# Where the hidden tiles' transposing transfers and joining copies stand in a streamed FFN, and where the rotation table lives

## The chip, the cores and the metric

One core of a Trainium2 chip runs the whole block as one program. The metric is the device time of one execution, in microseconds. Before the change it is 2484.98 us, the median of three runs between 2484.42 and 2486.36.

## The reference

One transformer layer over 256 rows of width 2048, everything in float32:

```python
h = layer_norm(ALPHA * h + 0.5 * swiglu_ffn(h, ffn1_w_in[l], ffn1_w_out[l]), ...)
mix = hybrid_mixer(h, w_in[l], gate_bias[l], rel_bias[l], ..., cos, sin)
h = layer_norm(ALPHA * h + mix, ...)
xa = memory_cross_attention(h, mem, ...)
h = layer_norm(ALPHA * h + xa, ...)
h = layer_norm(ALPHA * h + 0.5 * swiglu_ffn(h, ffn2_w_in[l], ffn2_w_out[l]), ...)
...
def swiglu_ffn(x, w_in, w_out):
    g, u = jnp.split(x @ w_in, 2, axis=-1)
    return (jax.nn.silu(g) * u) @ w_out
```

The hidden width is 5504, 43 blocks of 128. The mixer holds a chunked attention and a latent attention whose queries and key are turned by a rotation table (`cos`, `sin`).

## The kernel before

**Streaming the weights.** All weights come from HBM once. SyncE (SP) loads tiles `raw` of 128 x 2048 float32, 1 MB each, into three buffers (line 185). Each matmul operand is a pair: ScalarE (ACT) rounds the tile into `hi`, in two instructions of 1024 columns (line 248, in `halves`), VectorE (DVE) subtracts to get the rest, `lo` (line 251), and TensorE (PE) multiplies hi by hi, hi by lo and lo by hi, summing in PSUM. A tile `raw` is free for the next load when VectorE's subtraction has read it.

**An in-group of the FFN.** `ffn` (from line 534) goes over the hidden width in groups of four blocks of 128 columns; `F_SPLIT` makes two halves of 24 and 19 blocks, so six groups and then five, the last of which is 384 columns wide rather than 512. A group makes gate and up for 256 rows in `pair_group`, in eight steps numbered 0 to 7, each with a weight tile of its own. Steps 0, 1, 3, 5 and 7 are plain: 24 matmuls of `mm_pair` (line 295). Steps 2, 4 and 6 are *sums steps* (`mm_sums`, line 349): 21 matmuls over sums of weights (made by VectorE, lines 233 and 235, in a block called `H` and rounded into a block called `X`) into four PSUM banks of their own. After step 6 `shared` (lines 651 to 656) empties these banks: two copies of ScalarE, then two adds, a subtraction and another add or subtraction of VectorE; the next group's plain banks and sums banks trade places with them, so the next group's step 0 writes into the banks that `shared` has emptied.

**The hidden tile's way.** At the group's end `product` (in `hidden`) adds the sums results to the plain banks, takes SiLU and multiplies; the product is 256 x 512. It has to become a matmul operand, so it must be transposed. Per 128 rows (`tt` = 0, 1): ScalarE copies the float32 words apart into upper and lower 16-bit halves (line 709), a transposing transfer turns them (line 711, a DMA that ScalarE issues into its own queue, q10), and later `turn` joins the halves again (the *join*, line 716, on ScalarE) and splits the result into hi and lo of a block `H` (lines 240 and 241). After the six, and after the five groups, the out phase multiplies these H blocks with `w_out`.

**The order of the work.** The program is a list of items. `weave` puts side items between the main items of a group: `turn` of the group before stands ahead of main item 3 of the next group (or of the out phase, after a half's last group). Counted in main items, `shared` is one of them, so item 3 is step 3. `run` goes through the list and issues loads, roundings and subtractions of weights ahead of their use; a priority then places instructions within each engine's order, which is fixed when the program is built:

```python
self.weave(main, {3: [turn]} if turn else {}, prio=0)     # an in-group
...
side = {3: [turn]}                                        # an out phase
```

**The rest.** The first group of the first FFN takes the input from other loads; `load_rest` (line 515) then loads `h`, `vecs` and the rotation table `rope` (128 x 512 float32, 256 KB) on SP's queue at the third group. `rope` stays in a constant tile to the end and is read in two places of the mixer: `kpe` (lines 948, 949) and `rope_q` (line 1048). Work tiles `w2` of 128 x 512 words have five buffers; the product, its halves and the four results of `shared` are such tiles.

Of the kernel before, what the change touches and what calls it, by code (L numbers as in the profile page):

```python
# [94 lines left out]
class Kernel:  # L95
# [32 lines left out]
    def w2(self, shape=(P, 512), dt=F32):  # L128
        return self.work.tile(list(shape), dt, tag="w2", bufs=5, name=self.name("w2"))

# [41 lines left out]
    def run(self):  # L172
# [44 lines left out]

        done = 0
        for fn, ws, held, prio in self.items:
            need = done + len(ws)  # L220
            while nxt < len(queue) and ahead(need, held):
                live += slots(queue[nxt])
                ready.append(load(nxt))
                nxt += 1
            got = [ready.pop(0) for _ in ws]
            live -= sum(slots(queue[done + i]) for i in range(len(ws)))
            done = need
            with self.prio(prio):
                fn(*got)
# [13 lines left out]
    def halves(self, src, hi, lo):  # L243

        n = src.shape[1]
        for c in range(0, n, 1024):
            d = min(c + 1024, n)
            self.nc.scalar.copy(hi[:, c:d], src[:, c:d])  # L248

        with self.tc.issue_after(self.chain.ins) if self.chain is not None else nullcontext():  # L250
            self.nc.vector.tensor_tensor(lo[:, :n], src, hi[:, :n].bitcast(F32), ALU.subtract)  # L251
        return hi, lo
# [194 lines left out]
    def setup(self):  # L447
        nc, t = self.nc, self.t
        self.ones = self.w1((P, P))
        nc.vector.memset(self.ones, 1.0)  # L450
        nc.scalar.activation(self.sm("first", 1, bufs=1), self.ones[:, 0:1], AF.Silu)
        self.vecs = self.const.tile([P, N_VEC], F32, name="vecs")
        self.rope = self.const.tile([P, 2, S], F32, name="rope")
        self.ident = self.const.tile([P, P], F32, name="ident")
        make_identity(nc, self.ident)
        self.mask = self.const.tile([P, 3 * P], F32, name="mask")
        nc.gpsimd.memset(self.mask, 0.0)
        self.mask_out(self.mask)
        self.krope = self.const.tile([P, 2, S], F32, name="krope")
        nc.gpsimd.memset(self.krope, 0.0)  # L460
        self.h = [self.res.tile([P, D], F32, tag=f"h{i}", name=f"h{i}") for i in range(2)]
# [53 lines left out]
    def load_rest(self):  # L515
        nc, t = self.nc, self.t
        with self.tc.issue_after(self.last_load.ins):
            for tt in range(2):
                nc.sync.dma_start(self.h[tt], t["x"][tt])
            nc.sync.dma_start(self.vecs, t["vecs"])  # L520
            nc.sync.dma_start(self.rope, t["rope"])

# [8 lines left out]
    def ffn(self, tag, xT, st, first=None, steps=None, late=None, before=None, tags=None):  # L531
# [6 lines left out]
        for half, nf in enumerate(F_SPLIT):  # L538
# [3 lines left out]
            for g in range(-(-nf // 4)):  # L542
# [9 lines left out]
                else:  # L552
                    src = t[tag + "_w_in"][j] if n == 4 else t[tag + "_w_in_r"][0]
                    main = self.collect(self.pair_group, bank, src, n * P, KT, xT, SUMS_IN, fx, ps, qs, None, SUM_HOME + ("H5",))
                self.weave(main, {3: [turn]} if turn else {}, prio=0)
                for c, (home, _) in homes.items():
# [24 lines left out]

            side = {3: [turn]}
            for c, (home, k) in homes.items():
                if home == "X0":
                    side[4 + 2 * k] = [form(c)]
            if not end:
# [101 lines left out]
    def hidden(self, ps, j, g, n, hid, qs):  # L688
# [4 lines left out]
        def words(v):  # L693
            return v.bitcast(U16)

        def product():
            for tt in range(2):
# [7 lines left out]
                else:  # L705
# [4 lines left out]
                               words(s[tt]).rearrange("p (c k) -> p k c", k=2))  # L710
                nc.scalar.dma_start_transpose(words(s[tt]).rearrange("p (b q) -> p b q", q=P), words(u[tt]))

        def turn():
            hid.blocks += self.act([f"H{g}"]).blocks
            for tt in range(2):
                nc.scalar.copy(words(u[tt]).rearrange("p (c k) -> p k c", k=2),
                               words(s[tt]).rearrange("p (k c) -> p k c", k=2))
                hi, lo = (hid.blk(a, 4 * g, n)[:, :, tt * P:(tt + 1) * P] for a in (0, 1))
                self.split(u[tt].rearrange("p (i q) -> p i q", i=n), hi, lo)
        return product, turn  # L720

# [103 lines left out]
    def mixer(self, xT, st, steps):  # L825
# [109 lines left out]
        def kpe(w):  # L935
            both = w[0].rearrange("p (k m) -> p k m", k=KT)
            with self.prio(SOON):
                nc.scalar.copy(both[:, :, 64:], w[1].rearrange("p (k m) -> p k m", k=KT)[:, :, 64:].bitcast(F32))
            ps = self.at_tile()
            for kt in range(KT):  # L940
# [6 lines left out]
            swap(c, a, nc.gpsimd)  # L947
            nc.vector.tensor_tensor(a, a, self.rope[:, 0, :], ALU.mult)
            nc.vector.tensor_tensor(c, c, self.rope[:, 1, :], ALU.mult)
            for j in range(2):  # L950
# [80 lines left out]

        rope_items = []
        for g in range(2):
            def fn(w, g=g):
                if g == 0:
                    self.rt = self.block("T0")
                for j in range(4):
                    ps = self.mm_tile()
# [3 lines left out]
            def rope_q(g=g):  # L1042
# [4 lines left out]
                for v, k in ((r, 0), (sw, 1)):  # L1047
                    nc.vector.tensor_tensor(v, v, self.rope[:, k:k + 1, :].to_broadcast([P, 4, S]), ALU.mult)
                nc.vector.tensor_tensor(r, r, sw, ALU.add)
# [476 lines left out]
```

## Time and profile before

| what | value |
|---|---|
| median of three runs | 2484.98 us |
| the profiled execution | 2484.44 us |
| its span in the trace | 2482.6 us |
| mean granted clock of TensorE | 0.996 |
| busy time of TensorE | 2450.8 us, 99% of the span |
| busy time of VectorE | 2096.0 us, 84% |
| busy time of ScalarE | 1449.5 us, 58% |
| busy time of GpSimd (POOL) | 36.0 us, 1% |
| moved by the DMA engines | 501.42 MB, 202 GB/s |

The span runs from the first instruction to the last; the execution's own time is 1.84 us longer. Busy time counts instructions that compute; issuing a DMA and waiting do not count. An engine name with a q (ACTq, SPq) is the sequencer of that engine, where it issues DMAs. In lists of waits, an arrow with a name after idle time says what ended it. The granted clock is the share of its full rate at which TensorE was let run in a stretch of time.

### The profile page before, as it was taken

Reading aid. Unit: us, or ns where it says so; the run is one execution under the profiler, and the core shown is the slowest. Engines: PE = TensorE matmul, PEld = TensorE weight load, DVE = VectorE, ACT = ScalarE, POOL = GpSimd, SP = SyncE. Lnnn points to the kernel's source line nnn. Section 1 sums busy time; section 2 is a strip of 40 time slices with the busy share of each in tenths; the row PEclk is TensorE's granted clock in tenths of the full one; section 3 lists DMA queues with packets and bytes.
Section 4 is the critical chain, followed back from the end, with each engine's and each line's share of the span. In section 5 each row is a group of like instructions: output and inputs, shape, how many; then the busy total and the mean of one; then the engine's idle time right before and its main releaser. Section 6 shows DMA issues by size and latency. Waiting matters only on the chain.

```text
span 2482.6 us, 30056 instructions
## 1 busy us (share of the span) xinstructions
PE 2450.8 (99%) x11603; PEld 2052.7 (83%) x11603; DVE 2096.0 (84%) x2392; ACT 1449.5 (58%) x1932; POOL 36.0 (1%) x78
## 2 busy tenths in 40 slices
PE   9999999999999999999999999999999999999998
PEld 7788888888888888888888888898888888888976
DVE  8899989998878897788788798558878999889986
ACT  6667655766555556556455565545566665566652
POOL 0000000000000001000000000000000000000000
PEclk9999999999999999999999999999999999999999
DMA  7767556667645666554466557544556765666764
GB/s 265 222 220 207 197 203 228 209 202 194 230 177 203 212 212 210 183 165 152 163 232 223 187 174 250 187 161 152 196 195 204 229 216 208 220 202 211 243 191 142
DMA packets 118528, 501.42 MB, mean 202 GB/s; under 512 B 53904, under 2 KB 54672, under 8 KB 63216
## 3 DMA queue, kind: packets, MB, share of 16 engines
q1 hardware_dynamic: 67632, 468.94, 55.2%
q10 hardware_dynamic: 46304, 12.46, 3.1%
q0 software_dynamic: 4448, 18.09, 2.2%
q8 instruction: 91, 1.49, 0.2%
q14 instruction: 53, 0.43, 0.0%
HBM read 484.77 MB, written 2.10 MB: 196 GB/s over the span
## 4 chain that ended last, share of the span: by engine, by line
PE 91%; DVE 3%; DMA 3%; ACT 2%; issue 1%; ACTq 0%; DVEq 0%
PE mm L295 23%; PE at L295 23%; PE mm L349 10%; PE at L349 10%; PE mm L261 9%; PE mm L282 7%; PE mm L263 4%; DMA w<-w 2%; PE at L976 1%; PE at L282 1%; DVE lo L251 1%; ACT hi L248 1%; DVE X L251 1%; PE at L815 0%; PE at L1017 0%
## 5 line engine op out<-in xcount | busy, mean ns | idle before, releaser
L248 ACT CAST hi<-raw 128x1024 fp32r<-128x1024 f32 (+1 forms) x852 | 803.9, 984 | 529.8 <-PE at L295 175.5
L251 DVE TENSOR_TENSOR lo<-raw,hi 128x2048 fp32r<-128x2048 f32 (+1 forms) x427 | 905.5, 2122 | 197.4 <-ACT hi L248 194.7
L295 PE MATMUL mm<-hi,T 128*128 128x512 f32 (+1 forms) x1232 | 286.3, 383 | 0.0
L295 PEld LDWEIGHTS mm<-hi,T 128*128 128x128 f32 x1232 | 229.1, 188 | 43.3 <-DVE w L656 0.4
L295 PE MATMUL at<-hi,T 128*128 128x512 f32 x1072 | 255.8, 389 | 1.1 <-ACT hi L248 1.1
L248 ACT CAST X<-H 128x1024 fp32r<-128x1024 f32 (+1 forms) x166 | 170.2, 1034 | 139.4 <-DVE H L233 86.9
L295 PEld LDWEIGHTS at<-hi,T 128*128 128x128 f32 x1072 | 201.0, 188 | 43.8 <-ACT hi L248 2.0
L251 DVE TENSOR_TENSOR X<-H,X 128x2048 fp32r<-128x2048 f32 (+1 forms) x83 | 186.9, 2252 | 56.9 <-ACT X L248 56.0
L295 PE MATMUL at<-hi,H 128*128 128x512 f32 x592 | 144.5, 396 | 9.0 <-ACT hi L248 7.5
L295 PE MATMUL mm<-lo,T 128*128 128x512 f32 (+1 forms) x616 | 147.8, 382 | 0.0
L295 PEld LDWEIGHTS at<-hi,H 128*128 128x128 f32 x592 | 113.1, 192 | 34.4 <-ACT hi L248 8.4
L295 PE MATMUL at<-lo,T 128*128 128x512 f32 x536 | 133.0, 389 | 1.4 <-DVE lo L251 1.4
L295 PEld LDWEIGHTS mm<-lo,T 128*128 128x128 f32 x616 | 114.6, 188 | 20.9
L261 PE MATMUL mm<-T,hi 128*128 128x512 f32 x512 | 123.7, 393 | 0.0
L295 PEld LDWEIGHTS at<-lo,T 128*128 128x128 f32 x536 | 100.5, 188 | 22.6 <-DVE lo L251 1.8
L235 DVE TENSOR_TENSOR H<-H,raw 128x512 f32<-128x512 f32 (+1 forms) x166 | 112.5, 678 | 1.9
L261 PEld LDWEIGHTS mm<-T,hi 128*128 128x128 f32 x512 | 93.8, 188 | 19.1 <-issue 0.7
L295 PE MATMUL mm<-hi,H 128*128 128x512 f32 x448 | 108.0, 391 | 0.0
L233 DVE TENSOR_TENSOR H<-raw 128x1024 f32<-128x1024 f32 (+1 forms) x83 | 99.6, 1200 | 6.4 <-DMA raw<-ffn_w_in 5.4
L295 PEld LDWEIGHTS mm<-hi,H 128*128 128x128 f32 x448 | 83.6, 188 | 17.2 <-DVE w L270 0.2
L349 PE MATMUL mm<-X,X 128*128 128x512 f32 x348 | 92.4, 391 | 0.4 <-DVE X L251 0.4
L349 PE MATMUL at<-X,X 128*128 128x512 f32 (+1 forms) x315 | 82.0, 387 | 2.8 <-DVE X L251 2.8
(330 smaller groups left out, 4048.0 us busy)
## 6 DMA issues: line engine op xcount, KB each, us to landing
raw<-ffn_w_in SPq DMA_DIRECT2D x150, 1024.0 KB, 4.9
raw<-ffn_w_out SPq DMA_DIRECT2D x66, 1024.0 KB, 4.8
raw<-w_gate SPq DMA_DIRECT2D x32, 1024.0 KB, 4.8
raw<-ffn_w_out_r SPq DMA_DIRECT2D x16, 1024.0 KB, 4.9
raw<-w_qk SPq DMA_DIRECT2D x16, 1024.0 KB, 4.8
raw<-w_o_b SPq DMA_DIRECT2D x16, 1024.0 KB, 4.8
raw<-w_out SPq DMA_DIRECT2D x16, 1024.0 KB, 4.9
raw<-w_xk SPq DMA_DIRECT2D x16, 1024.0 KB, 4.9
```

The lines of the kernel that those rows point to most:

```text
L233: self.nc.vector.tensor_tensor(two[0], two[1], raw[:, :m].unsqueeze(1).to_broadcast([P, 2, m]), ALU.add)
L235: self.nc.vector.tensor_tensor(t[:, a * m:a * m + m], t[:, b * m:b * m + m], raw[:, a * m:a * m + m], ALU.add)
L248: self.nc.scalar.copy(hi[:, c:d], src[:, c:d])
L251: self.nc.vector.tensor_tensor(lo[:, :n], src, hi[:, :n].bitcast(F32), ALU.subtract)
L261: self.nc.tensor.matmul(ps, hi[j], x.both(kt), start=(j == 0), stop=False)
L263: self.last_mm = self.nc.tensor.matmul(ps[:, :S], lo[j], x.at(0, kt), start=False, stop=(j == n - 1))
L282: self.last_mm = self.nc.tensor.matmul(ps, x.at(xi, kt)[:, tt * P:(tt + 1) * P], w[wi][:, j * 512 + c:j * 512 + c + m], start=(start and j ...
L295: self.last_mm = self.nc.tensor.matmul(ps[tt, g][:, :n], x.at(xi, kt)[:, tt * P:(tt + 1) * P], w[wi][:, c:c + n], start=first and j + wi + ...
L349: self.last_mm = self.nc.tensor.matmul(bank[:, :m], a[xi], v[wi][:, c * m:(c + 1) * m], start=own and first and wi + xi == 0, stop=own and ...
L976: nc.tensor.matmul(ps[:, c0:c0 + nk], q[:, tt * P:(tt + 1) * P], k[:, :nk], start=(j == 0), stop=(j == len(parts) - 1))
```

## The change

It has three parts.

1. **The transposing transfers** leave `product` for an item of their own, `send`, that stands ahead of main item 2 of the next group, and SP issues them (line 719 of the new kernel) into the queue of the weight loads (q1), not ScalarE into q10.
2. **`turn`** moves from ahead of main item 3 to ahead of main item 6, which is step 6. Each of its joins (now line 725) is also ordered behind the last rounding of the weight that the next main item uses, `next_hi`; where that item is step 6, this is the seventh weight of the group, and the last rounding is that of its sums (into a block `X`). In the out phases `send` and `turn` take the same places 2 and 6 among other main items.
3. **The rotation table** loses its constant tile and its load in `load_rest`. `rotation()` takes a `w2` tile and has GpSimd load the 256 KB into it, once in `kpe` and once for each of the two rotation items of the queries. `w2` gets a sixth buffer.

Other line numbers rise by two to five: the rounding is line 250, its subtraction 253, the split into H 242 and 243, the plain matmuls 297, the sums matmuls 351, `shared` 656 to 661, the copy apart 714.

```diff
-        return self.work.tile(list(shape), dt, tag="w2", bufs=5, name=self.name("w2"))
+        return self.work.tile(list(shape), dt, tag="w2", bufs=6, name=self.name("w2"))
...
-        done = 0
+        done, highs = 0, []
         for fn, ws, held, prio in self.items:
             need = done + len(ws)
             while nxt < len(queue) and ahead(need, held):
                 live += slots(queue[nxt])
                 ready.append(load(nxt))
+                highs.append(self.last_hi)
                 nxt += 1
             got = [ready.pop(0) for _ in ws]
             live -= sum(slots(queue[done + i]) for i in range(len(ws)))
             done = need
+            self.next_hi = highs[min(done, nxt - 1)] if highs else None
...
-            self.nc.scalar.copy(hi[:, c:d], src[:, c:d])
+            self.last_hi = self.nc.scalar.copy(hi[:, c:d], src[:, c:d])
...
-            nc.sync.dma_start(self.rope, t["rope"])
+
+    def rotation(self):
+        r = self.w2((P, 2, S))
+        self.nc.gpsimd.dma_start(r, self.t["rope"])
+        return r
...
-                self.weave(main, {3: [turn]} if turn else {}, prio=0)
+                self.weave(main, turn or {}, prio=0)
...
-            side = {3: [turn]}
+            side = dict(turn)
             for c, (home, k) in homes.items():
                 if home == "X0":
-                    side[4 + 2 * k] = [form(c)]
+                    side[4 + 2 * k] = side.get(4 + 2 * k, []) + [form(c)]
...
-                nc.scalar.dma_start_transpose(words(s[tt]).rearrange("p (b q) -> p b q", q=P), words(u[tt]))
+
+        def send():
+            for tt in range(2):
+                nc.sync.dma_start_transpose(words(s[tt]).rearrange("p (b q) -> p b q", q=P), words(u[tt]))
 
         def turn():
             hid.blocks += self.act([f"H{g}"]).blocks
             for tt in range(2):
-                nc.scalar.copy(words(u[tt]).rearrange("p (c k) -> p k c", k=2),
-                               words(s[tt]).rearrange("p (k c) -> p k c", k=2))
+                with self.tc.issue_after(self.next_hi.ins):
+                    nc.scalar.copy(words(u[tt]).rearrange("p (c k) -> p k c", k=2),
+                                   words(s[tt]).rearrange("p (k c) -> p k c", k=2))
                 hi, lo = (hid.blk(a, 4 * g, n)[:, :, tt * P:(tt + 1) * P] for a in (0, 1))
                 self.split(u[tt].rearrange("p (i q) -> p i q", i=n), hi, lo)
-        return product, turn
+        return product, {2: [send], 6: [turn]}
```

In `kpe` and `rope_q` the reads of `self.rope` become reads of the tile that `rotation()` returned, called at the start of `kpe`'s work and of each query projection item.

The built programs show what stands where on each engine (line, operation, output<-input, tile shape of a partition count and a count of elements; `x2` is two such rows in a row). **First place**: ScalarE between the second group's product and the third group's weights. `hi_844`, `hi_880`, `hi_916` of before (`hi_840`, `hi_876`, `hi_914` now) are the roundings of the third group's weights of steps 2, 3 and 4, `w_108` to `w_111` hold the second group's product and its halves, `H_138` is its H block, and `X_123` takes the rounded weight sums. Before:

```order
L709 COPY w_108_753<-w_109_754 128x1024
L709 COPY w_110_755<-w_111_756 128x1024
L711 DMA_TRANSPOSE w_109_754<-w_108_753 128x8x128
L711 DMA_TRANSPOSE w_111_756<-w_110_755 128x8x128
L248 CAST hi_844<-raw_794 128x1024
L248 CAST hi_844<-raw_794 128x512
L248 CAST X_123_849<-H_116_796 128x1024 x2
L716 COPY w_108_753<-w_109_754 128x2x512
L248 CAST hi_880<-raw_878 128x1024 x2
L240 CAST H_138_926<-w_108_753 128x4x128
L716 COPY w_110_755<-w_111_756 128x2x512
L248 CAST hi_916<-raw_885 128x1024
```

and now:

```order
L250 CAST hi_840<-raw_793 128x1024
L714 COPY w_108_752<-w_109_753 128x1024
L250 CAST hi_840<-raw_793 128x512
L714 COPY w_110_754<-w_111_755 128x1024
L250 CAST X_123_845<-H_116_795 128x1024
L250 CAST hi_876<-raw_874 128x1024 x2
L250 CAST X_123_845<-H_116_795 128x1024
L250 CAST hi_914<-raw_881 128x1024
L250 CAST hi_914<-raw_881 128x512
```

The two issues and the two joins with their first split have left this place; the copies apart stand among roundings. SP at the same place, from the load of `raw_794` (now `raw_793`) on; before:

```order
L185 DMA raw_794<-ffn_w_in 128x2048
L519 DMA h_102<-x 128x2048
L519 DMA h_103<-x 128x2048
L520 DMA vecs<-vecs 128x136
L521 DMA rope<-rope 128x512
L185 DMA raw_878<-ffn_w_in 128x2048
L185 DMA raw_885<-ffn_w_in 128x2048
L185 DMA raw_957<-ffn_w_in 128x2048
```

and now:

```order
L185 DMA raw_793<-ffn_w_in 128x2048
L520 DMA h_101<-x 128x2048
L520 DMA h_102<-x 128x2048
L521 DMA vecs<-vecs 128x136
L185 DMA raw_874<-ffn_w_in 128x2048
L185 DMA raw_881<-ffn_w_in 128x2048
L719 DMA_TRANSPOSE w_109_753<-w_108_752 128x8x128
L719 DMA_TRANSPOSE w_111_755<-w_110_754 128x8x128
L185 DMA raw_948<-ffn_w_in 128x2048
```

The table's load is gone and the two transposing transfers stand between the loads of two weights. **Second place** on ScalarE and VectorE, **the third piece shown**: the end of step 6 in the fifth group, where `shared` (copies of `w_251` and `w_252`) now meets the joins of the group before (`w_203` to `w_206`, into `H_247`). `X_243` (now `X_242`) are the rounded sums of step 6, `hi_1652` (now `hi_1643`) is the rounding of step 7's weight, `hi_1680` (now `hi_1678`) and `hi_1721` (now `hi_1719`) are those of steps 0 and 1 of the next group. ScalarE before:

```order
L248 CAST X_243_1621<-H_240_1591 128x1024
L248 CAST hi_1652<-raw_1650 128x1024
L248 CAST X_243_1621<-H_240_1591 128x1024
L248 CAST hi_1652<-raw_1650 128x1024
L248 CAST hi_1680<-raw_1678 128x1024
L651 COPY w_251_1685<-at_1516 128x512
L248 CAST hi_1680<-raw_1678 128x1024
L652 COPY w_252_1686<-at_1517 128x512
L248 CAST hi_1721<-raw_1719 128x1024 x2
```

and now:

```order
L250 CAST X_242_1612<-H_239_1582 128x1024
L250 CAST hi_1643<-raw_1641 128x1024
L725 COPY w_203_1371<-w_204_1372 128x2x512
L656 COPY w_251_1683<-at_1514 128x512
L242 CAST H_247_1648<-w_203_1371 128x4x128
L725 COPY w_205_1373<-w_206_1374 128x2x512
L250 CAST hi_1678<-raw_1676 128x1024
L657 COPY w_252_1684<-at_1515 128x512
L242 CAST H_247_1648<-w_205_1373 128x4x128
L250 CAST hi_1678<-raw_1676 128x1024
L250 CAST hi_1719<-raw_1717 128x1024 x2
```

Two joins and two roundings into H are new beside the two copies, and one half of `hi_1678` comes later than the half of `hi_1680` did. VectorE now, behind the subtraction of step 7's weight:

```order
L253 TENSOR_TENSOR lo_1644<-raw_1641,hi_1643 128x2048
L243 TENSOR_TENSOR H_247_1648<-w_203_1371,H_247_1648 128x4x128
L658 TENSOR_TENSOR w_253_1685<-w_251_1683,at_1516 128x512
L659 TENSOR_TENSOR w_252_1684<-w_252_1684,w_253_1685 128x512
L243 TENSOR_TENSOR H_247_1648<-w_205_1373,H_247_1648 128x4x128
L660 TENSOR_TENSOR w_253_1685<-w_253_1685,at_1517 128x512
L661 TENSOR_TENSOR w_254_1686<-w_252_1684,at_1517 128x512
L253 TENSOR_TENSOR lo_1679<-raw_1676,hi_1678 128x2048
```

The two splits into H (line 243) are new here and stand ahead of the first add and between the second and the third of the four instructions that empty the banks. The joins stand at such a place in 18 of the 22 groups; the other four are in the out phases, where the blocks of a half's last group are joined.

More of the change, by code (lines that the diff above doesn't have):

```diff
@@ L452, in setup @@
         self.vecs = self.const.tile([P, N_VEC], F32, name="vecs")
-        self.rope = self.const.tile([P, 2, S], F32, name="rope")
         self.ident = self.const.tile([P, P], F32, name="ident")
@@ L938, in kpe @@
                 nc.scalar.copy(both[:, :, 64:], w[1].rearrange("p (k m) -> p k m", k=KT)[:, :, 64:].bitcast(F32))
+            rope = self.rotation()
             ps = self.at_tile()
@@ L947, in kpe @@
             swap(c, a, nc.gpsimd)
-            nc.vector.tensor_tensor(a, a, self.rope[:, 0, :], ALU.mult)
-            nc.vector.tensor_tensor(c, c, self.rope[:, 1, :], ALU.mult)
+            nc.vector.tensor_tensor(a, a, rope[:, 0, :], ALU.mult)
+            nc.vector.tensor_tensor(c, c, rope[:, 1, :], ALU.mult)
             for j in range(2):
@@ L1029, in a_out @@
             self.add(fn)
-        rope_items = []
+        rope_items, rot = [], {}
         for g in range(2):
@@ L1036, in fn @@
                     self.rt = self.block("T0")
+                rot[g] = self.rotation()
                 for j in range(4):
@@ L1047, in rope_q @@
                 for v, k in ((r, 0), (sw, 1)):
-                    nc.vector.tensor_tensor(v, v, self.rope[:, k:k + 1, :].to_broadcast([P, 4, S]), ALU.mult)
+                    nc.vector.tensor_tensor(v, v, rot[g][:, k:k + 1, :].to_broadcast([P, 4, S]), ALU.mult)
                 nc.vector.tensor_tensor(r, r, sw, ALU.add)
```

## The prediction

> **What bounds the kernel now.** I read the page first, then the waits of TensorE, then the lines that send and use the moved transfers, then the timeline around them. The page comes first: busy time, share of the span, instruction count, and below it the shares of the chain that ended last.
>
> ```profile
> span 2482.6 us, 30056 instructions
> PE 2450.8 (99%) x11603; PEld 2052.7 (83%) x11603; DVE 2096.0 (84%) x2392; ACT 1449.5 (58%) x1932; POOL 36.0 (1%) x78
> PE 91%; DVE 3%; DMA 3%; ACT 2%; issue 1%; ACTq 0%; DVEq 0%
> ```
>
> TensorE is the bound: it is idle for 2482.6 - 2450.8 = 31.8 us only. An edit on ScalarE or on a queue can therefore win only what lies in these idle places, and in matmuls that ran slowly behind them. The change touches one line with a wait of its own, the transposing transfers (line 711), which the joining copies (line 716) wait for:
>
> ```profile
> L711 ACTq DMA_TRANSPOSE w<-w x44: 1227/1249/2820, 56.1 to 2371.7; - x44
>   ACT w L716: 26.9, 9
> DMA to landing us min/median/max: 3.0/4.4/16.6
> ```
>
> Issuing one holds ScalarE for about 1.25 us, it lands after 3.0 to 16.6 us, and ScalarE stands 26.9 us before joins. Does TensorE pay for that? The timeline (start, duration, engine, line; in brackets the idle time before it and who ended it) shows three places where it does, and two plain pieces to compare with:
>
> ```profile
> 109.13 3.79 PE L295 MATMUL mm<-hi,T 128*128 128x512 f32 x16
> 115.11 1.33 ACT L716 COPY w<-w 128x1024 uint16<-128x1024 uint16 x1 [6.58 <-DMA w<-w]
> 117.92 0.73 PE L349 MATMUL mm<-hi,T 128*128 128x512 f32 x2 [3.18 <-ACT hi L248]
> 125.96 3.80 PE L295 MATMUL mm<-hi,T 128*128 128x512 f32 x16
> ...
> 216.64 0.62 PE L349 MATMUL mm<-hi,T 128*128 128x512 f32 x2
> 221.40 3.79 PE L295 MATMUL mm<-hi,T 128*128 128x512 f32 x16
> ...
> 613.81 1.04 ACT L716 COPY w<-w 128x768 uint16<-128x768 uint16 x1 [7.13 <-DMA w<-w]
> 616.63 5.54 PE L295 MATMUL at<-hi,H 128*128 128x512 f32 x16 [4.18 <-ACT hi L248]
> 2388.43 5.51 PE L295 MATMUL at<-hi,H 128*128 128x512 f32 x16 [3.35 <-ACT hi L248]
> ```
>
> ScalarE waits 6.58 and 7.13 us for a transpose, the rounding (line 248) of the next weight is queued behind that join, and TensorE waits for this rounding. Sixteen matmuls then take 5.54 and 5.51 us where 3.79 is usual, and the sums step from 117.92 lasts until 125.96, 8.04 us, where the one from 216.64 lasts 4.76. The windows of these stretches (columns: length, busy time and count of each engine, granted clock, DMA share, GB/s) say why:
>
> ```profile
> 118.70:122.10 3.40, 3.40 (x9) 2.58 (x8) 3.36 (x5) 2.19 (x3) 0.00 (x0) 0.50 0.05 19
> 126.00:130.00 4.00, 4.00 (x19) 3.33 (x18) 4.00 (x4) 1.22 (x2) 0.00 (x0) 1.00 0.49 147
> 617.10:620.40 3.30, 3.30 (x10) 2.52 (x9) 3.15 (x4) 2.84 (x4) 0.00 (x0) 0.50 0.00 0
> 2388.60:2392.00 3.40, 3.40 (x9) 2.63 (x10) 3.25 (x4) 3.14 (x4) 0.00 (x0) 0.50 0.00 0
> ```
>
> After each of the three waits the granted clock is 0.50 for some 3.4 us and 1.00 afterwards, so each wait is paid about one and a half times.
>
> **Part 1, the three stalls.** Wait plus lengthening: 3.18 + (8.04 - 4.76) = 6.46 us; 4.18 + (5.54 - 3.79) = 5.93; 3.35 + (5.51 - 3.79) = 5.07. Together 17.46 us. In the new order no rounding is queued behind a join that still waits: the transposes go out behind the third step and the join stands behind the seventh weight's rounding, over four steps later. A plain step is 226.84 - 221.40 = 5.44 us (row below), so some 20 us lie between, more than the longest landing of 16.6. I book the whole 17.46.
>
> By the Trainium skill (TensorE: Matmul & The Clock Gate, HAM oscillation) idle gaps have to exceed about 3.4 us before the clock is halved. The trace differs: 3.18 and 3.35 us were enough. By the rule only the wait of 4.18 would have been charged the slow clock, and some 5 us of the sum would be of another origin and might stay.
>
> **Part 2, why the transposes were late, and whether SP's queue carries them.** Median landing of a weight load, the three loads issued from 98.9 to 110.4 us, the two queues, and what SP's queue waits for:
>
> ```profile
> raw<-ffn_w_in SPq DMA_DIRECT2D x150, 1024.0 KB, 4.9
> DMA to landing us min/median/max: 9.5/12.6/16.2
> q1 hardware_dynamic: 67632, 468.94, 55.2%
> q10 hardware_dynamic: 46304, 12.46, 3.1%
> SPq L185 <- DVE lo L251: 1503.8, 294, 15.3
> ```
>
> Beside the slow transposes the weight loads, usually 4.9 us, took 9.5 to 16.2: both wait on each other. The transposes of q10 are 46304 small packets (12.46 MB) that share the 16 DMA engines with q1. In one queue I take them to run one behind the other: 3.0 us each, the shortest landing. SP has room for the issues: it waits 1503.8 us in all for VectorE to free a raw tile. What stands behind them is the next weight load: at worst it is late by two issues (2.5 us) and two transposes (6.0 us). Below nothing too: a load no longer slowed from 4.9 to 16.2 gains up to 11.3 us. I take zero, nearest to the row of 4.9, since a load is late only after the joins have left ScalarE's way. The tightest place is the short last group (384 wide), where SP comes to the transposes before they are ready:
>
> ```profile
> L185 SPq DMA_DIRECT2D raw<-ffn_w_out x1: 328/328/328, 596.1 to 596.1; - x1
> 596.98 1.56 ACT L709 COPY w<-w 128x768 uint16<-128x768 uint16 x2
> ```
>
> That load must now follow copies that end at 598.54 and two issues, so it goes out near 600.5 and lands by 605.4 to 611.4 (0 or 6.0 us of transposes ahead of it). Its matmuls are those that would start at 616.63 - 4.18 = 612.45; rounding takes 2 us, so the stall is 0 to 1 us. I take 0.
>
> The Trainium skill (DMA: Bandwidth & Descriptors, Issuing engines are not separate DMA queues) speaks against a gain here: the issuing engine saves sequencer time only, and all transfers interleave on the same DMA engines. Its section on queues, rings and completion order says that a DMA engine takes turns between queues packet by packet but consumes one ring in order, which fits the rows above; by the first sentence alone the late loads would stay, which is the first rival.
>
> **Part 3, ScalarE without the issues.** 44 issues of 1.25 us leave ScalarE, 55 us, but it is 58% busy; only the first group shows TensorE behind them:
>
> ```profile
> 59.36 1.06 ACT L248 CAST X<-H 128x1024 fp32r<-128x1024 f32 x1 [2.33 <-issue]
> 61.41 1.20 PE L295 MATMUL at<-hi,T 128*128 128x512 f32 x4 [0.91 <-ACT hi L248]
> 67.49 0.72 PE L295 MATMUL at<-lo,T 128*128 128x512 f32 x2 [1.38 <-DVE lo L251]
> ```
>
> The 2.33 us go. Of the 0.91 + 1.38 = 2.29 us between 0 and 2.29 return, since VectorE's chain follows; I take 1.5.
>
> **Part 4, the joins in their new place.** They now meet the four copies and adds that empty the shared banks (lines 651 to 656 of before) between step 7's rounding and the next group's first step, in 18 of 22 groups. Rows of such a place, and the durations of a join copy and of the rounding into H:
>
> ```profile
> 217.69 2.00 ACT L248 CAST hi<-raw 128x1024 fp32r<-128x1024 f32 x2
> 219.59 0.58 ACT L651 COPY w<-at 128x512 f32<-128x512 f32 x1
> 220.03 2.28 DVE L251 TENSOR_TENSOR lo<-raw,hi 128x2048 fp32r<-128x2048 f32 x1
> 222.23 0.68 DVE L653 TENSOR_TENSOR w<-w,at 128x512 f32<-128x512 f32 x1
> 226.84 3.79 PE L295 MATMUL at<-hi,T 128*128 128x512 f32 x16
> ...
> L716 ACT COPY w<-w x44: 1043/1358/1373, 63.2 to 2385.6; 128x1024 uint16<-128x1024 uint16 x40, 128x768 uint16<-128x768 uint16 x4
> L240 ACT CAST H<-w x72: 401/612/634, 65.6 to 2386.9; 128x512 fp32r<-128x512 f32 x44, 128x256 fp32r<-128x256 f32 x24, 128x384 fp32r<-128x384 f32 x4
> ```
>
> In the new order (third place shown above) ScalarE, from the second half of step 7's rounding (done at 218.65): join 1.36, copy 0.58, H 0.61, join 1.36, half a rounding 1.0, copy 0.58, H 0.61, half a rounding 1.0, to 225.75. TensorE needs that first half, done at 223.6, at 226.84. VectorE, from 222.31: split 0.69, add 0.68, add (after the copy at 224.1) 0.69, split, add, subtract, to 226.9; TensorE enters the last of the four banks six matmuls, 1.36 us, after 226.84, at 228.20: 1.3 us are left. So zero for these groups. For the two 384-wide groups the step is 0.75 as long, 4.1 us, and the same work (two joins, two H, copy: 4.4 us) comes before the next rounding: I take 0.9 us each, 1.8, between 0 and 4.
>
> **Part 5, the rotation table.** One load of 256 KB leaves SP's queue, three are issued by POOL. Its nearest transfer and the table's use:
>
> ```profile
> w<-gb POOLq DMA_DIRECT2D x24, 256.0 KB, 4.5
> 1054.21 0.70 POOL L990 DMA_DIRECT2D X<-bias  x1 [8.91 <-issue]
> L1048 DVE TENSOR_TENSOR T<-T,rope x4: 1204/1218/1223, 1082.9 to 1089.2; 128x1024 f32<-128x1024 f32 x4
> ```
>
> POOL is free 28 us before the first multiplication and the load needs 4.5: zero, and 4.5 at most if no buffer is free. The sixth buffer pays for the table's space and costs nothing.
>
> **Sum.** 17.46 + 1.5 - 1.8 = 17.2 us. The profiled execution took 2484.44 us, its span and 1.84 around it, 0.5 below the median of 2484.98. Forecast: 2484.44 - 17.2 = 2467.3 us.
>
> **Rivals.**
> - *The loads stay late.* If transposes and loads still hold each other up in one queue, the stall at 117.9 us, whose load landed 16.2 us after issue, stays with 6.46 us: 2473.7, and near 2479 if another does. Against it: in q1 alone loads land in 4.9 us.
> - *The joins push the banks.* The last of the four banks is freed when both splits and the joins before them are done. Where the joins start 1.3 us late, each further microsecond is paid 18 times. From 1.26 us beyond that (22.7 us / 18) the kernel is slower than before by over 0.2%; at 2 us it takes 2467.3 + 36 = 2503. For it: VectorE is 84% busy. Against it: ScalarE is 58% busy and has 3 us left there.
> - *Part of that*, 0.7 to 1.25 us each, eats the gain: 2480 to 2490.
>
> **How the numbers follow.** Forecast (2460 to 2472, part 3 in full and part 4 at nothing or doubled): 0.64. Late loads (2472 to 2479): 0.14. Gain eaten: 0.12. Slower: 0.10. What this measurement can tell from no change is 0.2%, 5 us. So faster 0.78, same 0.12, slower 0.10. The range 2460 to 2482 leaves out the last case and most of the third.
>
> **What would show it.** Right: no wait of line 716's successor on a transfer, granted clock 1.00 at the three places, transposes on q1 landing in 3 to 6 us, loads near them under 9 us, TensorE's idle time near 20 us. Wrong: waits of TensorE for line 661's results or for the rounding at group boundaries, or a load over 9 us behind a transpose.

## The result

The changed kernel takes 2466.45 us, the median of six runs between 2465.59 and 2469.12; beside it the kernel before took 2485.67 us (2480.4 to 2487.52). The ratio is 0.9927, with a 95% interval of 0.9915 to 0.994. The forecast was 2467.3 us, in a range from 2460 to 2482. The profiled execution took 2466.44 us, 18.0 less than the one before, where the sum had 17.2.

The page after: span, busy times, the chain that ended last, and the two queues.

```profile
span 2464.7 us, 30068 instructions
PE 2445.8 (99%) x11603; PEld 2048.8 (83%) x11603; DVE 2093.3 (85%) x2392; ACT 1447.0 (59%) x1932; POOL 37.6 (2%) x81
...
q1 hardware_dynamic: 112928, 479.96, 57.4%
...
q10 hardware_dynamic: 864, 1.18, 0.1%
...
PE 94%; DVE 3%; ACT 1%; DMA 1%; issue 1%; DVEq 0%; SPq 0%; ACTq 0%
```

TensorE is now idle for 2464.7 - 2445.8 = 18.9 us where it was 31.8, and the transposes' small packets have gone from q10 to q1 (the 864 that stay on q10 are not theirs). The group of the transposing transfers says how they fare there:

```profile
L719 SPq DMA_TRANSPOSE w<-w x44: 1211/1232/3807, 56.3 to 2357.7; - x44
...
DMA to landing us min/median/max: 3.0/3.5/6.2
```

They land in 6.2 us at the latest instead of 16.6, and no engine is named as waiting for them: ScalarE's 26.9 us before the joins are gone. The timeline of TensorE at the three places where it stalled before:

```profile
111.02 0.61 PE L351 MATMUL mm<-hi,T 128*128 128x512 f32 x2
...
115.78 3.79 PE L297 MATMUL mm<-hi,T 128*128 128x512 f32 x16
...
603.02 3.79 PE L297 MATMUL at<-hi,H 128*128 128x512 f32 x16
...
2372.16 3.79 PE L297 MATMUL at<-hi,H 128*128 128x512 f32 x16
```

The sums step lasts 115.78 - 111.02 = 4.76 us instead of 8.04, the two pieces behind the other stalls take 3.79 instead of 5.54 and 5.51, and no row has idle time ahead of it. The windows there show the granted clock (the number behind the busy times of POOL) at 1.00:

```profile
112.00:116.00 4.00, 4.00 (x19) 3.26 (x18) 3.61 (x2) 2.78 (x4) 0.00 (x0) 1.00 0.52 219
600.00:604.00 4.00, 4.00 (x20) 3.30 (x19) 4.00 (x4) 2.48 (x3) 0.00 (x0) 1.00 0.46 139
2370.00:2374.00 4.00, 4.00 (x20) 3.30 (x19) 4.00 (x5) 1.62 (x3) 0.00 (x0) 1.00 0.68 225
```

What TensorE still loses in the FFNs lies in three places, by its own timeline and by ScalarE's:

```profile
585.43 2.11 PE L297 MATMUL at<-lo,H 128*128 128x512 f32 x8 [1.03 <-DVE lo L253]
...
2331.90 0.44 PE L297 MATMUL mm<-hi,T 128*128 128x384 f32 x1 [0.22 <-ACT hi L250]
2333.36 0.97 PE L351 MATMUL at<-X,X 128*128 128x384 f32 x4 [1.02 <-ACT X L250]
...
2342.00 0.61 PE L297 MATMUL mm<-hi,T 128*128 128x384 f32 x2 [0.20 <-ACT hi L250]
2343.46 0.96 PE L351 MATMUL at<-X,w 128*128 128x384 f32 x4 [0.85 <-ACT X L250]
...
2354.57 2.11 PE L297 MATMUL at<-lo,H 128*128 128x512 f32 x8 [0.99 <-DVE lo L253]
```

```profile
2305.06 1.35 ACT L725 COPY w<-w 128x1024 uint16<-128x1024 uint16 x1
...
2307.26 1.36 ACT L725 COPY w<-w 128x1024 uint16<-128x1024 uint16 x1
...
2330.80 1.57 ACT L250 CAST hi<-raw 128x1024 fp32r<-128x1024 f32 x2 [5.20 <-DMA raw<-ffn_w_in_r]
...
2340.90 1.57 ACT L250 CAST hi<-raw 128x1024 fp32r<-128x1024 f32 x2 [4.83 <-DMA raw<-ffn_w_in_r]
```

The two waits of about 1 us for `lo` stand at the starts of the last out phases, right behind the 384-wide groups. Between 2331.9 and 2346 the second FFN's 384-wide group waits for its loads.

To compare the kernels, I sum over TensorE's matmuls by how much two starts lie further apart than the plain spacing of that width (226.7 ns for 512 columns, the 5.44 us of a plain step by 24). This **lost time** holds waits and slow clocks alike, and the rest of the span is the same for all. The middle stands for mixer and cross attention.

Each row is of the one execution that was profiled. Two of these were slower than the median of their kernel: that of the rotation table alone (2489.0 us, median 2483.78) and that of the spread pairs (2473.75, median 2467.21).

| kernel | first FFN | middle | second FFN | all |
|---|---|---|---|---|
| before | 22.2 | 42.0 | 9.1 | 73.3 |
| changed | 6.9 | 42.7 | 5.9 | 55.4 |
| rotation table alone | 25.4 | 42.9 | 9.8 | 78.1 |
| queue alone | 5.0 | 43.9 | 5.2 | 54.1 |
| joins alone | 7.9 | 42.8 | 6.0 | 56.7 |
| pairs spread, joins at 3 | 15.8 | 43.3 | 3.7 | 62.8 |
| pairs back to back, joins at 6 | 22.3 | 44.7 | 16.0 | 83.0 |
| changed, joins at 4 | 4.0 | 42.7 | 1.2 | 47.8 |

Of each first FFN, 3.6 to 4.2 us are the program's start.

### The profile page after: what moved, and what is told of

It reads as the page before. It is cut to its first block, busy times and chain, and to the rows that moved or that the text cites. A ratio compares the mean times of both kernels' runs of the same rounds, so it can differ in the third digit from the quotient of the medians.

```text
span 2464.7 us, 30068 instructions
## 1 busy us (share of the span) xinstructions
PE 2445.8 (99%) x11603; PEld 2048.8 (83%) x11603; DVE 2093.3 (85%) x2392; ACT 1447.0 (59%) x1932; POOL 37.6 (2%) x81
## 4 chain that ended last, share of the span: by engine, by line
PE 94%; DVE 3%; ACT 1%; DMA 1%; issue 1%; DVEq 0%; SPq 0%; ACTq 0%
PE at L297 24%; PE mm L297 24%; PE at L351 10%; PE mm L351 10%; PE mm L263 9%; PE mm L284 7%; PE mm L265 4%; PE at L986 1%; PE at L284 1%; DVE lo L253 1%; DMA raw<-ffn_w_in_r 1%; PE at L824 1%; PE at L1027 0%; PE at L1346 0%; ACT hi L250 0%
## 5 line engine op out<-in xcount | busy, mean ns | idle before, releaser
L297 PEld LDWEIGHTS mm<-hi,H 128*128 128x128 f32 x448 | 83.6, 188 | 17.2 <-DVE w L272 0.2
L250 ACT CAST X<-raw 128x1024 fp32r<-128x1024 f32 (+1 forms) x54 | 55.3, 1034 | 50.9 <-DVE raw L237 36.9
```

Source lines behind the costliest of these rows:

```text
L250: self.last_hi = self.nc.scalar.copy(hi[:, c:d], src[:, c:d])
L297: self.last_mm = self.nc.tensor.matmul(ps[tt, g][:, :n], x.at(xi, kt)[:, tt * P:(tt + 1) * P], w[wi][:, c:c + n], start=first and j + wi + ...
```

## The experiments

Two theories stood at the outset. **A**: the stalls come from transfers of two queues that hold each other up. **B**: they come from roundings queued behind a join that waits. Kernels whose times are compared ran on one chip, beside the kernel before; across chips I compare the lost time. The edits are shown, shortened, as differences to the changed kernel.

### The rotation table alone

```diff
-                nc.sync.dma_start_transpose(...)
+                nc.scalar.dma_start_transpose(...)
...
-        return product, {2: [send], 6: [turn]}
+        return product, {3: [turn]}
```

The issues stand in `product` again and the joins have no order of their own; only the table's new load and the sixth buffer stay.

> The kernel before with the rotation table loaded by GpSimd at its use and six w2 buffers, transposes and joins as before. Both theories: within 3 us of the kernel before, 2482 to 2488 us, since the table's 256 KB land long before they are read; a gain of over 5 us would mean that the table's load or the sixth buffer, and not the moves, carries part of the gain.

Measured: 2483.78 us beside 2482.38, ratio 1.0006 (0.9989 to 1.0022). Within this interval (some -3 to +5 us) the table and the buffer carry nothing. The stall of the second group is larger in this kernel's profile; TensorE's waits, in all, times and longest:

```profile
PE mm L351 <- ACT hi L250: 11.9, 1, 11.9
```

### The queue alone

```diff
-        def send():
-            for tt in range(2):
                 nc.sync.dma_start_transpose(...)
...
-                with self.tc.issue_after(self.next_hi.ins):
-                    nc.scalar.copy(...)
+                nc.scalar.copy(...)
...
-        return product, {2: [send], 6: [turn]}
+        return product, {3: [turn]}
```

SP issues the transposes in `product`, straight behind the copies; the joins have no order of their own.

> The changed kernel with one part undone: SP issues the transposing transfers, but straight behind the copies that feed them, and the joins stand ahead of main item 3 again, ordered behind nothing. Theory A (the three stalls come from transfers of two queues that share the DMA engines, so one queue is enough): transposes land in 3 to 7 us, the loads near them in under 9, no TensorE wait over 2 us in the three places, 2466 to 2469 us. Theory B (the stalls come from the roundings queued behind a waiting join, so the joins must move): the joins at step 3 still wait some us for their transfers and at least two of the three waits of TensorE stay at 2 us or more, 2474 to 2482 us.

Measured: 2463.01 us beside 2482.38, ratio 0.9911 (0.9891 to 0.9932), still below A's range. The three stalls are gone with the joins still at step 3. From the kernel with the rotation table alone this one differs only in the queue and the engine that issues.

### The joins alone

```diff
-                nc.sync.dma_start_transpose(...)
+                nc.scalar.dma_start_transpose(...)
...
-        return product, {2: [send], 6: [turn]}
+        return product, {6: [turn]}
```

ScalarE issues the transposes in `product` again.

> The changed kernel with the other part undone: ScalarE issues the transposing transfers into its own queue straight behind the copies, as before the change; the joins stand ahead of main item 6 behind the rounding, as after it. Theory A (late transfers of two queues): the loads near the three places still land 10 to 16 us after issue; by the times of the trace before, they land 1.5, 2.5 and 1.7 us too late for TensorE once the rounding's 1.05 us is added, so 5.7 us of the 17.5 stay, and the first group's 3.8 us too: 2472 to 2477 us. Theory B (roundings behind the join): the three places lose nothing, the first group's 3.8 us stay, 2468 to 2471 us.

Measured: 2469.79 us beside 2482.38, ratio 0.9939 (0.9922 to 0.9956). The three stalls are gone here too, as B had it. But its loads were not late either, which neither theory had said. The issues in a window around the second group's transposes (count, KB, median us to landing) show it, in the kernel before,

```profile
raw<-ffn_w_in SPq DMA_DIRECT2D x3, 1024.0 KB, 12.6
w<-w ACTq DMA_TRANSPOSE x2, 10.9
```

with the rotation table alone,

```profile
raw<-ffn_w_in SPq DMA_DIRECT2D x3, 1024.0 KB, 22.0
w<-w ACTq DMA_TRANSPOSE x2, 18.1
```

with the queue alone,

```profile
raw<-ffn_w_in SPq DMA_DIRECT2D x4, 1024.0 KB, 5.1
w<-w SPq DMA_TRANSPOSE x2, 4.1
```

and with the joins alone:

```profile
raw<-ffn_w_in SPq DMA_DIRECT2D x4, 1024.0 KB, 5.4
w<-w ACTq DMA_TRANSPOSE x2, 5.2
```

Two queues are at work in the last of these as in the first two, yet nothing is late. What differs is ScalarE's order: with the joins out of the way, the scheduler put a rounding or a copy between the two issues of this pair, 3.4 us apart instead of 1.3. The out phases' pairs are still 1.3 us apart and nothing is late there either (6.2 us at most): the next load was issued 0.04 us behind the second transpose, in the kernel before 0.33 us. So the experiment had changed more than the joins, and two later ones try to take this apart. As no transpose landed late at the three places, it doesn't show that moved joins alone would remove the stalls beside late ones.

### The item ahead of step 2, issued by ScalarE

```diff
-                nc.sync.dma_start_transpose(words(s[tt])...
+                nc.scalar.dma_start_transpose(words(s[tt])...
```

> The changed kernel with a single word changed: the item ahead of main item 2 issues the transposes on ScalarE's queue, not on SP's. Theory A (two queues): transposes up to 16 us and loads of 9 to 16 us come back, TensorE waits 1 to 3 us in two or three places, 2471 to 2477 us. Theory B (roundings behind the join): only the issues on ScalarE return, 44 of 1.25 us, mostly covered: 2467 to 2470 us.

Measured: 2469.1 us beside 2482.38, ratio 0.9953 (0.9931 to 0.9975), in B's range. No transpose landed later than 9.9 us; here, too, most pairs were issued 1.8 to 3.9 us apart, and the out phases' pairs had the next load 0.04 us behind.

### Pairs spread, joins at step 3

```diff
+                if tt == 0:
+                    nc.scalar.dma_start_transpose(...)
...
+        def send():
+            with self.tc.issue_after(self.last_hi.ins):
+                nc.scalar.dma_start_transpose(...)
...
-        return product, {2: [send], 6: [turn]}
+        return product, {1: [send], 3: [turn]}
```

> Transposes on ScalarE's queue and joins ahead of main item 3 as before the change, but the second transpose of a pair is issued behind a rounding of the next step in 20 of 22 groups; the pairs of the two out phases stay back to back. Theory A (a pair in flight together is what is slow): at the first of the three places the second transpose lands in 3 to 6 us and TensorE waits under 1 us there, while the two places of the out phases keep waits of 3 us or more: 2474 to 2480 us. Theory B (a join at step 3 is simply too early): the first place keeps a wait of 2 us or more as well, 2480 to 2486 us.

Measured: 2467.21 us beside 2482.66, ratio 0.9945 (0.9928 to 0.9962), faster than either theory had it. The profile is of the slowest execution, 2473.75 us; whether the faster ones have the same losses is not shown. In it the second group's pair is 2.4 us apart, the second transpose lands after 8.6 us, and the place loses 2.4 us instead of 6.5. Its waits of 0.6 and 1.3 us lie between A's and B's. The pair of the first FFN's out phase is still back to back, and there the old stall stands unchanged: ScalarE's and TensorE's timeline, and the landings of the second transposes.

```profile
606.64 1.05 ACT L726 COPY w<-w 128x768 uint16<-128x768 uint16 x1 [5.06 <-DMA w<-w]
```

```profile
609.24 3.35 PE L297 MATMUL at<-hi,H 128*128 128x512 f32 x7 [3.58 <-ACT hi L250]
```

```profile
DMA to landing us min/median/max: 3.0/4.7/14.3
```

The 14.3 is this pair's. One execution thus shows both cases, a spread pair with a smaller loss and a back-to-back pair with the stall, both with joins at step 3. The second FFN's pair, back to back too, landed in 11.6 us, but TensorE lost only 1.1 us there.

### Pairs back to back, joins at step 6

```diff
-                nc.scalar.copy(...)
+                last = nc.scalar.copy(...)
+            with self.tc.issue_after(last.ins):
+                for tt in range(2):
+                    nc.scalar.dma_start_transpose(...)
...
-        return product, {2: [send], 6: [turn]}
+        return product, {6: [turn]}
```

> As the run with the joins alone moved, but ScalarE issues both transposes of all 22 groups back to back behind both copies (in that run 17 pairs had a rounding or a copy between them). Theory A (two transposes in flight together beside a weight load of the other queue hold each other up): second transposes land 8 to 17 us after issue in most groups that have a load right behind, the loads in 9 to 16 us; since the joins no longer wait, TensorE pays only for the late loads, 1 to 3 us in some places: 2472 to 2480 us. Theory B (only roundings queued behind a waiting join cost time): the slow landings may come back, but the time stays at that run's, 2467 to 2471 us.

Measured: 2493.96 us beside 2482.66, ratio 1.0052 (1.0039 to 1.0065). It is outside both ranges, and slower than the kernel before although no join waits. The landings of 7 to 11 us did come back in some groups, but that isn't what it loses by. The group of the transposes, then ScalarE's and TensorE's timeline behind the fifth group's product:

```profile
L718 ACTq DMA_TRANSPOSE w<-w x44: 1227/1329/4168, 56.3 to 2382.1; - x44
...
DMA to landing us min/median/max: 2.7/5.9/11.3
```

```profile
226.97 1.05 ACT L714 COPY w<-w 128x1024 uint16<-128x1024 uint16 x1 [0.88 <-DVE w L708]
226.98 5.10 ACTq L718 DMA_TRANSPOSE w<-w  x2
232.12 1.05 ACT L250 CAST X<-H 128x1024 fp32r<-128x1024 f32 x1 [4.10 <-issue]
```

```profile
235.12 0.73 PE L351 MATMUL mm<-X,X 128*128 128x512 f32 x2 [0.71 <-ACT X L250]
```

Two issues back to back hold ScalarE for 5.10 us, not 2.5, where they meet a load already under way; the rounding of the weight sums stands behind them and TensorE waits for it. In all, ScalarE's waits of such roundings for an issue grew from 3.7 us, twice, to 22.8, six times:

```profile
ACT X L250 <- issue: 22.8, 6, 4.1
```

The places where TensorE loses time in the FFNs number eighteen behind the program's start, 0.7 to 3.9 us each; that the issue is behind every one of them is not shown. So issues on ScalarE can cost time where the order leaves no room behind them.

### The joins of one group taken from the boundary

```diff
                 hidden, turn = self.hidden(ps, bank, g, n, hid, qs)
+                if end and g == 2:
+                    turn = {2: turn[2], 4: turn[6]}
```

> The changed kernel with the joins of the third group of the second half moved from main item 6 to main item 4, so that they no longer stand at the boundary ahead of the 384-wide last group. If those joins push the roundings, and through them the loads, of the last group: of the 4.0 us that TensorE loses between 2331 and 2347 us at least 2.5 go, 2462 to 2465 us where the changed kernel has 2466. If the last group is bound by the bandwidth of its loads, with GpSimd's loads beside them: the 4 us stay within 1 us.

Measured: 2469.26 us beside 2482.66, ratio 0.995 (0.9937 to 0.9963). The time is above the forecast, and of the 4.0 us in the last group 2.2 stay, between the two expectations. The losses at the starts of the two last out phases grow from 1.3 to 2.1 us each. Two executions of one kernel (below) differ by as much in that group, so this run decides nothing about it.

### The changed kernel with all joins at step 4, beside itself

```diff
-        return product, {2: [send], 6: [turn]}
+        return product, {2: [send], 4: [turn]}
```

> The changed kernel once more, unaltered, on the same chip as the next three, as their measure. Both theories: 2464 to 2469 us, and again 1.3 us of TensorE's time lost at the start of each FFN's last out phase and 3 to 4 us in the second FFN's 384-wide group.

> The changed kernel with one number changed: the joins stand ahead of main item 4, not 6. If the joins at the group boundaries cost what was booked for them (the two 384-wide groups and the places behind them), both losses of 1.3 us at the starts of the last out phases go and the loss in the second FFN's last group falls from 4.0 to under 1.5: 2 to 5 us below the changed kernel. If the boundary is innocent, the losses stay and the time is within 1 us of it.

Measured: the changed kernel 2466.42 us, with joins at step 4 2459.44 (2457.35 to 2460.43, below every run of the other), beside 2480.76 for the kernel before; ratios 0.9944 (0.9927 to 0.9962) and 0.9914 (0.9897 to 0.9931). The changed kernel again loses 1.3 us at each of the two out phases, and 3.2 in the last group. With joins at step 4 all of these are gone. All waits of TensorE that the profile lists with joins at step 4:

```profile
PE at L475 <- DVE w L452: 1.1, 1, 1.1
PE mm L284 <- ACT T L242: 0.4, 1, 0.4
PE mm L284 <- DVE T L243: 0.4, 1, 0.4
PE at L1027 <- ACT w L830: 0.2, 1, 0.2
```

None of them is a wait within an FFN's groups. This is the fastest version measured, 7.0 us below the changed kernel, more than the 5 that I had expected at most.

### Transposes straight behind the copies, on SP, joins at 4 and at 6

```diff
-        return product, {2: [send], 6: [turn]}
+        return product, {4: [turn]}
```

> SP issues the transposes straight behind the copies, as in the run with the queue alone, and the joins stand ahead of main item 4, ordered behind nothing. With transfers of 3 to 7 us the joins have landed data a step earlier than they need it, and they stand at no group boundary: the 8.9 us that ScalarE waited for transfers in that run go, TensorE loses under 4 us in both FFNs where that run lost 4.8: 2460 to 2464 us. If the place of the joins matters beside the queue by more than that, it is under 2460 or over 2466.

Measured: 2462.45 us beside 2482.66, ratio 0.9927 (0.9915 to 0.9939).

> The run with transposes by SP straight behind the copies and joins ahead of main item 4 once more, beside the changed kernel on one chip: both theories have it 2 to 5 us below the changed kernel, since it loses nothing at the boundaries; within 1 us of it would mean that the difference between the earlier runs lay in the chips.

> SP issues the transposes straight behind the copies, as in the runs of the queue alone and of the queue with joins at item 4, and the joins stand ahead of main item 6 behind the rounding, as in the changed kernel. If the joins' place is what the changed kernel loses by: the two losses of 1.3 us and those of the last group are back, 2464 to 2467 us. If the place of the transposes behind step 2 is what it loses by: these losses are gone, 2461 to 2463.5 us.

Measured on the chip of the changed kernel's 2466.42: joins at 4, 2463.42 us; joins at 6 behind the rounding (`{6: [turn]}`), 2467.14. With joins at 6 both losses of 1.3 us at the out phases are back, and 4.1 us in the last group; with joins at 4 the out phases lose nothing, and the last group 1.2 in one profile and 3.1 in the other. So the place of the joins makes the losses at the out phases, wherever the transposes stand. What makes those in the last group stays open: the queue alone, with joins at 3, loses 2.7 us there too. Why transposes behind step 2 with joins at 4 ordered behind the rounding do 4 us better than transposes straight behind the copies with joins at 4 ordered behind nothing stays open as well.

## Why the prediction was right, and where it was off

**The three stalls (17.46 us) go.** By the lost time they were 6.55, 6.07 and 5.22, together 17.84, and none is left. The reason given, that no rounding is queued behind a waiting join any more, is true of the changed kernel, but it is not what its gain needs: the queue alone, with the joins at step 3 and free, removed all three stalls (54.1 lost). Curing the late landings was enough. The joins alone had no stall either (56.7 lost), but no late landing to stand up to, and the spread pair cut its stall from 6.5 to 2.4 us. Each of these stalls, before and in the runs that kept one, had two transposes of ScalarE's queue back to back, a weight load 0.3 to 0.5 us behind the second one and a join at step 3; but in the kernel before, eight pairs had all of this and only three stalled. That moving the queue alone would gain as much as all three parts was not foreseen.

**The transposes in one queue run in 3 us each, and loads gain nothing.** They land in 3.0 to 6.2 us; the forecast for q1 was 3 to 6. The first rival, that loads stay late, fell. That loads gain nothing was wrong: the four near the second group's pair land in 5.3 to 7.3 us, where three took 9.5 to 16.2. The rate of the DMA engines (last column, GB/s) in windows of the kernel before, from the second group's transposes on, says how they were late:

```profile
98.00:100.00 2.00, 2.00 (x10) 1.66 (x9) 2.00 (x2) 0.13 (x1) 0.00 (x0) 1.00 1.08 449
100.00:104.00 4.00, 4.00 (x20) 3.30 (x19) 2.41 (x4) 2.58 (x4) 0.00 (x0) 1.00 1.61 194
104.00:108.00 4.00, 4.00 (x19) 3.30 (x18) 3.07 (x2) 4.00 (x5) 0.00 (x0) 1.00 1.05 102
108.00:112.00 4.00, 4.00 (x19) 3.33 (x18) 2.29 (x1) 0.53 (x2) 0.00 (x0) 1.00 0.58 110
112.00:116.00 4.00, 2.74 (x13) 1.92 (x11) 0.76 (x1) 0.89 (x1) 0.00 (x0) 1.00 1.04 414
```

and after the change:

```profile
99.00:103.00 4.00, 4.00 (x19) 3.33 (x18) 3.94 (x4) 3.93 (x5) 0.00 (x0) 1.00 1.08 293
103.00:107.00 4.00, 4.00 (x20) 3.30 (x19) 4.00 (x3) 1.00 (x2) 0.00 (x0) 1.00 1.07 326
```

For some twelve us the engines moved 102 to 194 GB/s with one to three loads under way; in one queue they move 293 to 326. The transfers did not merely share the rate of 449 and 414 GB/s on either side, they lost some two thirds of it. The Trainium skill (DMA: Bandwidth & Descriptors, Issuing engines are not separate DMA queues) has the issuing engine save sequencer time only. These runs differ: the queue alone is worth 20.8 us (2483.78 with the rotation table alone, 2463.01 with the queue besides); of these, 3.8 us are the first group's two places (next paragraph), which go back to ScalarE's issues.

**ScalarE without the issues: 1.5 us was too small.** The first group's two places had lost 2.17 and 1.66 us; nothing is left of either, 3.8 us.

**The joins in their new place: -1.8 us was the term most mis-sized.** For the 18 groups at a boundary zero was right; no wait for line 661 is left, and the second rival fell. The two 384-wide groups were booked at 0.9 each and cost 1.3 each, at the start of the out phase behind. The further 4.0 us in the second FFN's last group were not booked: its loads come late. All joins at step 4 take both away. That the joins ahead of this group delay its first roundings, thus the release of raw tiles and the next loads, is what the timeline suggests; the run that moved one group's joins removed only half, and the queue alone loses 2.7 us there without joins at a boundary, so this chain is argued, not shown.

**Gains that were not booked.** Small waits in groups with joins at step 3 (0.65, 1.37 and 0.84 us lost at 157, 212 and 1982 us) and one behind the second FFN's last group (2.03 at 2363), 4.9 in all, are gone.

Together: 17.8 + 3.8 + 4.9 - 2.6 - 4.0 = 19.9 us; the measured difference of 18.0 is 1.9 less, of which 0.5 is a longer wait at the transposes of the first layer norm and the rest pieces under 0.4 us. That the forecast met the time within 0.8 us is luck: an unforeseen loss and unforeseen gains nearly balanced.

**The rotation table** costs nothing, as forecast.

## What to carry to other kernels

When a transfer lands late, look at what else is in flight from other queues in those microseconds before moving its consumer: here the rate of the DMA engines fell to a third, and issuing the transposes in the queue of the loads cured it without moving the joins. Then look where the moved work has come to stand: a place right at a boundary between groups, where banks are emptied and the next weights rounded, cost 7 us that a place two steps earlier did not. And when an edit lets a scheduler reorder an engine, compare the orders before giving the edit the credit.

## What the runs showed of the hardware

- Two DMA transposes issued 1.3 to 1.4 us apart on ScalarE's queue, with a 1 MB load of SP's queue issued 0.3 to 0.5 us behind the second one, were late in all 19 such pairs of these profiles: the second landed after 8.2 to 16.6 us, 24.5 in one case, and the load after 7.2 to 24.2. With the load 0.04 us behind the second one (four pairs, at the out phases of the joins alone and of `send` on ScalarE) it landed after 6.1 to 7.5.
- Spread by 2.9 us or more, transposes of ScalarE's queue landed in 3 to 7.1 us, with two exceptions of 9.2 and 9.9. Back to back is not enough to be late: in the run with all pairs back to back, where a load was issued 0.6 us ahead of the pair and the next one 5.4 us behind its start, both landed in 5.4 to 6.7; where the next one came 2.9 us behind it, the second took 8.0 to 11.3. What within the DMA engines causes it stays open.
- Issuing a transpose takes 1.25 us in the median, but up to 4.17 on ScalarE (all pairs back to back) and 3.81 on SP (the changed kernel); the two shown above that took 5.10 met a load already under way.
